# High/low splits of the block products' operands: all subtractions on VectorE, none on GpSimd

## The chip, the cores and the metric

One core of a Trainium2 chip runs the whole program. The metric is the device time of one execution in microseconds (us); shorter is better. The engines are named as in the profile: PE is TensorE's matrix multiply (PEld its weight load), DVE is VectorE, ACT is ScalarE, POOL is GpSimd, SP is the engine whose queue issues most DMAs. Every engine works through its own list of instructions in order; semaphores make it wait for the others.

## The reference

Two layers over 1024 tokens of width 1024, float32, batch 1. Cut to what matters here:

```python
# layer 0: convolution branch and bidirectional RG-LRU branch, then one output projection
z = h @ p["w_in"]                                   # 1024 -> 5 * 1024
y = concat([y_a, y_b], axis=-1) @ p["w_out"]        # 2048 -> 1024
x = x + gate * y
# layer 1: multi-scale pooling mixer
u, g = split(h @ p["w_in"], 2)                      # 1024 -> 2 * 2048
d = multiscale_pool(u)                              # windows 2, 4, 8, 16 along rows of 64 tokens
y = einsum("bngi,gij->bngj", d, p["w_grp"]) * p["scale"]
x = x + gate * ((y * silu(g)) @ p["w_out"])
return rmsnorm(x, final_g)
```

## The kernel before, in words

Features lie on the 128 partitions, tokens along the free axis. TensorE multiplies fp32r operands. To keep float32 accuracy, every operand v is split in two: hi is a copy of v rounded to fp32r, made on ACT, and lo = v - hi, a subtraction (`TENSOR_TENSOR`, line 96) on VectorE or GpSimd. A product is then three matmuls per pair of 128x128 weights and 128x512 data: hi\*hi, hi\*lo, lo\*hi.

From about 764 us to the end of the trace the kernel does "block products", which save multiplications by Strassen's method. Two output rows of 128 features are taken together. Their weights are four blocks a11, a12, a21, a22 (each 128x512), and `wquad` builds seven weight operands `wq_*` from them with one sum and three differences on DVE (L587, L588, L589, L595) and seven splits. The data are cut the same way into b11, b21, b22, t1, t2, t3, t4 (`block_sums` on DVE, L559 to L562). `quad` then runs seven products p1 to p7 (84 matmuls, lines L607, L609, L610) into three PSUM tiles a, c and b. Tile b begins as a copy of a, made on ACT (L625). Results leave PSUM in parts: an ACT copy for a first part, a DVE addition for the second (L1022 and L1030 for the pooling layer, L833, L1077 and L1092 for the output projections). The last product p4 (operand t4) may start adding to b only when DVE has read the part before it.

The order of the products is p1 (b11), p5 (t1), p6 (t2), p2 (b21), p7 (t3), p3 (b22), p4 (t4). The stages are:

- `woa`, 4 quads, about 764 to 862 us: layer 0's output projection. Its data operands `ya` are split by `split_op`.
- about 862 to 906 us: products `fold` of weights for layer 1, normalisation, and the start of the operands `x_*` (`split_x`).
- `v` and `g`, 8 steps of two quads each, about 906 to 1256 us: the pooling input (`v`) and its gate (`g`). In each step DVE also does the pooling sums of two feature rows and two token halves (`pool`: L928 sums, L937 and L941 edges, L946), the gate product (L1062), the block sums of the result, and in four steps two reductions of a 512 KB modulation tile (L206), loaded from DRAM.
- `wo0` and `wo1`, about 1256 to 1446 us: layer 1's output projection in two halves. Its data operands are loaded back from DRAM and split by `y_operand`, 128x1024 at a time.

Which engine subtracts was fixed by hand: in a `wquad` weights 1 and 6 on DVE, weights 2, 3, 4, 5 and 7 on GpSimd; of the data operands about every second one on GpSimd. The raw weights `wr` have two buffers, just one pair, so the next pair is loaded when the splits 3 and 4, the last readers, are done. The order on each engine is set by the framework's scheduler, which plays the program against its own timing model; evictions of PSUM get a raised priority. Changing an engine therefore also reorders the lists.

Of the kernel before, what the change touches and what calls it, by code (L numbers as in the profile page):

```python
# [22 lines left out]
HALF = (slice(0, H), slice(H, S))  # L23
# [32 lines left out]
def body(ctx, tc, xT, ctxT, cc, ccol, modT, modW, win, gw, wout, wu, grp, wg, wo1, small, edge, ident, outT):  # L56
    nc = tc.nc
# [23 lines left out]
    def ttile(name):  # L81
        return tpool.tile([P, H], F32, tag="t", name=name)
# [11 lines left out]
    def split(src, hi, lo, eng):  # L94
        return (nc.scalar.copy(hi, src),  # L95
                eng.tensor_tensor(out=lo, in0=src, in1=hi.bitcast(F32), op=sub))  # L96
# [324 lines left out]
    with ExitStack() as actx:  # L421
# [6 lines left out]
        def ltile(name, dt=F32):  # L428
            return lpool.tile([P, E], dt, tag="l", name=name)
# [49 lines left out]
        for j in range(KT):  # L479
# [15 lines left out]
            for h in range(2):  # L495
                ps = psum(f"vg{j}_{h}")
                mm3(ps, w, (hh, hl), HALF[h])
                t = ttile(f"sg{j}_{h}")
# [16 lines left out]
            for d in range(2):  # L515
                for gi, ob in ((0, O_BR), (1, O_BI)):
                    kc = slice((2 * gi + d) * P, (2 * gi + d + 1) * P)
                    t = ltile(f"g{j}_{d}_{gi}")
# [21 lines left out]
    def vtile(name):  # L540
        return vpool.tile([P, H], F32, tag="v", name=name)
# [10 lines left out]

    def split_op(ops, name, i, src):
        hi, lo = ops[name]
        return split(src, hi[i], lo[i], nc.gpsimd if i % 2 else nc.vector)


    def block_sums(b11, b12, b21, b22, t3, eng):
        eng.tensor_tensor(out=t3, in0=b22, in1=b12, op=sub)  # L559
        eng.tensor_tensor(out=b12, in0=b12, in1=b11, op=sub)  # L560
        eng.tensor_tensor(out=b11, in0=b22, in1=b12, op=sub)
        eng.tensor_tensor(out=b21, in0=b21, in1=b11, op=sub)  # L562
        return dict(t2=b11, t1=b12, t3=t3, t4=b21, b22=b22)
# [5 lines left out]
    def wquad(src, name, ring, late=False):  # L569
        raw = []  # L570
        for i in range(2):
            r = wpool.tile([P, D], F32, tag="wr", name=f"wr_{name}_{i}")
            loaded[0] = nc.sync.dma_start(r, src[i])
            raw.append(r)
        a11, a12 = [raw[0][:, h] for h in HALF]
        a21, a22 = [raw[1][:, h] for h in HALF]

        def op(v, i, eng):
            t = ring(f"wq_{name}_{i}")
            split(v, t[:, HALF[0]], t[:, HALF[1]], eng)  # L580
            return t

        p1 = op(a11, 1, nc.vector)
        if late:
            p4 = op(a22, 4, nc.gpsimd)
        s3 = ttile(f"ws_{name}")
        nc.vector.tensor_tensor(out=s3, in0=a11, in1=a21, op=sub)  # L587
        nc.vector.tensor_tensor(out=a21, in0=a21, in1=a22, op=add)  # L588
        nc.vector.tensor_tensor(out=a11, in0=a21, in1=a11, op=sub)  # L589
        if not late:  # L590
            p5 = op(a21, 5, nc.gpsimd)
        p6 = op(a11, 6, nc.vector)
        p2 = op(a12, 2, nc.gpsimd)
        p7 = op(s3, 7, nc.gpsimd)
        nc.vector.tensor_tensor(out=a12, in0=a12, in1=a11, op=sub)  # L595
        if late:
            p5 = op(a21, 5, nc.gpsimd)
        p3 = op(a12, 3, nc.gpsimd)
        if not late:
            p4 = op(a22, 4, nc.gpsimd)  # L600
        return p1, p2, p3, p4, p5, p6, p7

    def prod(ps, w, op, first, last):
# [109 lines left out]
    for h in range(2):  # L713
        ps = wide(f"mu{h}", h)[:, :H]
        nc.tensor.matmul(ps, ones, lnacc[h][:, :H], start=True, stop=True)
        for j in range(KT):
            v = us[j][:, HALF[h]]
# [3 lines left out]
            else:  # L721
                q = ttile(f"lsq{j}_{h}")
                nc.scalar.activation(q, v, AF.Square)
                eng = nc.gpsimd if h else nc.vector
# [5 lines left out]
    for m in range(KT):  # L730
        w = wload(wout[m, 1], f"wob{m}", nc.gpsimd)
        for h in range(2):
            ps = psum(f"wob{m}_{h}")
            mm3(ps, w, (bh, bl), HALF[h])
            t = vtile(f"xp{m}_{h}")
# [36 lines left out]
    for i in range(KH):  # L772
        for j in (i, KH + i):
            w = wload(win[2 * KT + j], f"ga{j}", nc.gpsimd)
            for h in range(2):
                ps = psum(f"ga{j}_{h}")
                mm3(ps, w, (hh, hl), HALF[h])
                nc.scalar.activation(ps, ps, AF.Silu)
                v = us[j][:, HALF[h]]
                nc.vector.tensor_tensor(out=v, in0=v, in1=ps, op=mult)  # L780
        b11, b12 = [us[i][:, h] for h in HALF]
        b21, b22 = [us[KH + i][:, h] for h in HALF]
        split_op(ya, "b11", i, b11)
        split_op(ya, "b21", i, b21)
        t1, t2, t3, t4 = b11, ttile(f"yat2_{i}"), b12, b21
        nc.vector.tensor_tensor(out=t1, in0=b12, in1=b11, op=sub)
        nc.vector.tensor_tensor(out=t3, in0=b22, in1=b12, op=sub)
        nc.vector.tensor_tensor(out=t2, in0=b22, in1=t1, op=sub)
        nc.vector.tensor_tensor(out=t4, in0=b21, in1=t2, op=sub)
        split_op(ya, "t2", i, t2)  # L790
        split_op(ya, "t1", i, t1)
        for name, v in zip(BOPS[4:], (t3, b22, t4)):
            kept[name].append(v)
        for _ in range((6, 6, 4, 0)[i]):
            next(mods)
# [9 lines left out]
    def wo_weights(m):  # L805
        return wquad([wout[m + i, 0] for i in range(2)], f"woa{m}", ring_w)
# [58 lines left out]
    def v_weights(m, ring):  # L865
        return wquad([wfold[(m + i) // 4][(m + i) % 4].rearrange("p k c -> p (k c)") for i in range(2)], f"v{m}", ring)
# [4 lines left out]
    def split_x(name, i, src, shift, eng):  # L871
        hi, lo = bx[name]
        if shift is None:
            split(src, hi[i], lo[i], eng)
        else:
            nc.scalar.activation(hi[i], src, AF.Identity, bias=shift)
            nc.vector.scalar_tensor_tensor(out=lo[i], in0=src, scalar=shift, in1=hi[i].bitcast(F32), op0=add, op1=sub)

    def scaled(h, k):
        v = x1[k][:, HALF[h]]  # L880
        nc.vector.scalar_tensor_tensor(out=v, in0=v, scalar=a1[:, 0, k : k + 1], in1=rs[h], op0=mult, op1=mult)
        return v

    def shift(k):
        return m1[:, 0, k : k + 1]
# [9 lines left out]
    for i in range(KH):  # L895
        b11, b21 = x1[i][:, HALF[0]], scaled(0, KH + i)
        split_x("b21", i, b21, shift(KH + i), None)
        b12, b22 = scaled(1, i), scaled(1, KH + i)
        t = block_sums(b11, b12, b21, b22, ttile(f"xt3_{i}"), nc.vector)
        split_x("t1", i, t["t1"], None, nc.gpsimd)  # L900
        split_x("t2", i, t["t2"], shift(KH + i), None)
        split_x("t3", i, t["t3"], dsh[:, i : i + 1], None)
        split_x("b22", i, b22, shift(KH + i), None)
        split_x("t4", i, t["t4"], None, nc.gpsimd)


    fin = [None, None]
# [63 lines left out]
    def y_operand(ops, part, name, raw_tile, alloc):  # L971
        hi, lo = [], []
        for q in range(2):
            r = raw_tile(f"yr_{part}_{name}_{q}")
            nc.sync.dma_start(r, y_raw[part][name][:, q * S : (q + 1) * S])
            hi.append(alloc(f"y{part}_{name}h{q}", F32R))
            lo.append(alloc(f"y{part}_{name}l{q}", F32R))
            split(r, hi[q], lo[q], nc.vector if q or name == "b22" else nc.gpsimd)
        halves = lambda ts: [t[:, h] for t in ts for h in HALF]
        ops[name] = halves(hi), halves(lo)  # L980

# [2 lines left out]
    def y_operands(part, raws, names=BOPS, alloc=None):  # L984
        for name in names:
            y_operand(yops[part], part, name, next(raws),
                      alloc or (dtile if name in ("b11", "b21", "t4") else d2tile))
# [11 lines left out]
    def wo1_weights(part, m):  # L999
        return wquad([wo1[m + i, part] for i in range(2)], f"wo{part}_{m}", wo1_ring,  # L1000
                     part == 1 and m >= KT - 4)
# [370 lines left out]
```

## Time and profile before

| | before |
|---|---|
| time, median of 3 runs | 1459.48 us (1458.37 to 1459.95) |
| the profiled execution: time, span | 1463.59 us, 1461.8 us |
| PE busy | 1320.6 us (90%) |
| DVE busy | 1220.5 us (83%), 1389 instructions |
| ACT busy | 653.0 us (45%) |
| POOL busy | 695.8 us (48%), 372 instructions |
| HBM traffic | 124 GB/s over the span |

The span runs from the first to the last instruction of the profiled execution. An engine's busy share over the whole span mixes stages with different limits; what the change is worth is read from 764 us on. A row "A line <- B line: us, times, longest" of the waits says that engine A, before the instruction named, was idle until engine B's instruction named was done. In grouped rows, x is the count, then follow total busy us and the mean ns of one.

### The profile page before, as it was taken

The numbers are of one execution on the slowest core, as the hardware profiler recorded it, in microseconds if no ns is written. First come the engines' busy times: TensorE is split into PE (matmuls) and PEld (weight loads), VectorE is DVE, ScalarE is ACT, GpSimd is POOL, SyncE is SP. The second block draws the span as 40 slices with busy tenths as digits, with TensorE's granted clock in tenths as the row PEclk, the third lists the DMA queues.
The fourth block names the chain that finished last, engine by engine and source line by source line (L and its number), as shares of the span: only waits on it lengthen the run. The fifth ranks groups of instructions, "written<-read, shape, count | busy, mean of one in ns | idle before, by whom it ended". The sixth has DMA issues, their size and how long they took to land. (4 is left out here: it accounts for less than half of the span.)

```text
span 1461.8 us, 15776 instructions
## 1 busy us (share of the span) xinstructions
PE 1320.6 (90%) x5664; PEld 1060.1 (73%) x5664; DVE 1220.5 (83%) x1389; ACT 653.0 (45%) x928; POOL 695.8 (48%) x372
## 2 busy tenths in 40 slices
PE   7889989998899899999998998899889998889796
PEld 4478767776777677788886776677767777668585
DVE  7985889799879899997778749999999887876765
ACT  6343674475467623225424345533333334534442
POOL 5183644663666556424427435543243344654522
PEclk9899999999999999999999999999999999999998
DMA  9731112111211133443545364233323235647623
GB/s 354 253 121 37 65 37 73 51 68 40 79 51 51 64 103 106 142 141 115 168 159 174 121 194 131 86 115 131 127 75 108 101 108 137 234 162 266 237 73 115
DMA packets 82866, 181.79 MB, mean 124 GB/s; under 512 B 7778, under 2 KB 27618, under 8 KB 82788
## 3 DMA queue, kind: packets, MB, share of 16 engines
q1 hardware_dynamic: 74340, 176.60, 35.6%
q10 hardware_dynamic: 8448, 4.20, 1.0%
q8 instruction: 44, 0.72, 0.2%
q14 instruction: 34, 0.28, 0.1%
HBM read 136.72 MB, written 44.04 MB: 124 GB/s over the span
## 5 line engine op out<-in xcount | busy, mean ns | idle before, releaser
L688 DVE SCALAR_TENSOR_TENSOR conv<-u,sm,conv 128x1009 f32<-128x1009 f32 (+14 forms) x240 | 301.0, 1273 | 21.7 <-ACT conv L681 18.5
L96 POOL TENSOR_TENSOR wq_v<-wr_v,wq_v 128x512 fp32r<-128x512 f32 x32 | 54.3, 1712 | 84.6 <-ACT wq_v L95 84.4
L96 POOL TENSOR_TENSOR wq_g<-wr_g,wq_g 128x512 fp32r<-128x512 f32 x32 | 49.8, 1567 | 91.8 <-ACT wq_g L95 91.5
L96 POOL TENSOR_TENSOR wq_wo<-wr_wo,wq_wo 128x512 fp32r<-128x512 f32 x32 | 49.1, 1542 | 58.4 <-ACT wq_wo L95 48.6
L96 POOL TENSOR_TENSOR wl_wu<-wr_wu,wh_wu 128x1024 fp32r<-128x1024 f32 x16 | 39.4, 2467 | 73.6 <-ACT wh_wu L95 73.6
L95 ACT CAST wq_g<-wr_g 128x512 fp32r<-128x512 f32 x48 | 28.2, 619 | 94.7 <-DVE wr_g L588 33.9
L95 ACT CAST wq_v<-wr_v 128x512 fp32r<-128x512 f32 x48 | 28.2, 619 | 81.0 <-DVE wr_v L595 29.3
L521 PE MATMUL g<-uh,wh_gw 128*128 128x512 f32 (+1 forms) x96 | 40.7, 425 | 25.8 <-ACT g L524 16.3
L524 ACT ACTIVATE g<-g,sm 128x512 f32<-128x512 f32 (+1 forms) x96 | 53.6, 624 | 18.0 <-PE g L523 10.0
L440 POOL TENSOR_TENSOR g<-g,uc 128x1280 f32<-128x1280 f32 x16 | 47.4, 2961 | 19.6 <-ACT g L524 19.6
L243 PE MATMUL fold<-gh,wh_wu 128*128 128x512 f32 x128 | 52.7, 413 | 4.3 <-ACT wh_wu L95 4.3
L125 PE MATMUL gb<-h0h,wh_gb 128*128 128x512 f32 x128 | 51.2, 400 | 5.7 <-ACT sb L669 5.7
L244 PE MATMUL fold<-gl,wh_wu 128*128 128x512 f32 x128 | 52.5, 410 | 3.2 <-DVE gl L96 3.2
L95 ACT CAST wq_wo<-wr_wo 128x512 fp32r<-128x512 f32 x48 | 28.8, 619 | 58.9 <-DVE wr_wo L588 15.0
L445 POOL TENSOR_TENSOR g<-g,g 128x1280 f32<-128x1280 f32 x16 | 50.6, 3182 | 9.1 <-ACT g L444 9.1
L446 DVE SCALAR_TENSOR_TENSOR g<-a,g 128x1280 f32<-128x1280 f32 x16 | 37.1, 2317 | 20.4 <-POOL g L445 20.4
L245 PE MATMUL fold<-gh,wl_wu 128*128 128x512 f32 x128 | 50.9, 407 | 2.7 <-POOL wl_wu L96 2.7
L928 DVE TENSOR_TENSOR ws<-ws 128x616 f32<-128x616 f32 (+2 forms) x48 | 52.3, 1091 | 0.9
L458 POOL TENSOR_TENSOR g<-g,g 128x1024 f32<-128x1024 f32 x8 | 19.2, 2394 | 70.6 <-DVE g L455 70.6
L127 PE MATMUL va<-h0h,wl_va 128*128 128x512 f32 x128 | 49.5, 391 | 2.1 <-POOL wl_va L96 2.1
L126 PE MATMUL gb<-h0l,wh_gb 128*128 128x512 f32 x128 | 51.0, 399 | 0.0
L127 PE MATMUL gb<-h0h,wl_gb 128*128 128x512 f32 x128 | 50.8, 398 | 0.0
(566 smaller groups left out, 4744.7 us busy)
## 6 DMA issues: line engine op xcount, KB each, us to landing
mod<-modT SPq DMA_DIRECT2D x28, 512.0 KB, 5.3
wr_wu<-wu SPq DMA_DIRECT2D x16, 512.0 KB, 4.1
x_part<-xp SPq DMA_DIRECT2D x32, 256.0 KB, 2.6
mod<-modT SPq DMA_DIRECT2D x32, 256.0 KB, 3.3
wr_v<-wfold SPq DMA_DIRECT2D x16, 512.0 KB, 3.3
wr_g<-wg SPq DMA_DIRECT2D x16, 512.0 KB, 4.3
yr_t<-y_t SPq DMA_DIRECT2D x16, 512.0 KB, 6.1
wr_wo<-wo SPq DMA_DIRECT2D x16, 512.0 KB, 4.2
```

The source lines that it names most:

```text
L95: return (nc.scalar.copy(hi, src), eng.tensor_tensor(out=lo, in0=src, in1=hi.bitcast(F32), op=sub))
L96: eng.tensor_tensor(out=lo, in0=src, in1=hi.bitcast(F32), op=sub))
L125: nc.tensor.matmul(ps, hi[:, kc], xh[k][:, cols], start=(k == 0), stop=False)
L126: nc.tensor.matmul(ps, hi[:, kc], xl[k][:, cols], start=False, stop=False)
L127: nc.tensor.matmul(ps, lo[:, kc], xh[k][:, cols], start=False, stop=(k == ks - 1))
L243: nc.tensor.matmul(ps, wh[:, kc], gh[i], start=(i == 0), stop=False)
L244: nc.tensor.matmul(ps, wh[:, kc], gl[i], start=False, stop=False)
L245: nc.tensor.matmul(ps, wl[:, kc], gh[i], start=False, stop=(i == 3))
L445: nc.gpsimd.tensor_tensor(out=iu, in0=iu, in1=r, op=mult)
L524: nc.scalar.activation(t[:, a : a + n], ps[:, :n], AF.Sigmoid, bias=col(ob + d * KT + j))
L688: nc.vector.scalar_tensor_tensor(out=acp[:, a:b], in0=us[j][:, a + o : b + o], scalar=col(O_CONVW + 31 * j + k), in1=acp[:, a:b], op0=mult ...
L928: nc.vector.tensor_tensor(out=nxt[:, :, a_:b_], in0=cur[:, :, a_ + o0 : b_ + o0], in1=cur[:, :, a_ + o1 : b_ + o1], op=add)
```

## The change

Every call of `split` in the block products gets VectorE: five of the seven weight splits of a `wquad`, the odd-numbered data operands of `woa`, the operands t1 and t4 of `v`/`g`, and the operands of `wo0`/`wo1` that GpSimd had. In all 174 subtractions move, 162 of 128x512 and 12 of 128x1024. The casts on ACT and the arithmetic stay, and no DMA is added or taken away. GpSimd's list goes from 371 to 197 rows: the earlier stages' work, the splits of `wl_wu`, eight small memsets and the last scaling stay there.

```diff
     def split_op(ops, name, i, src):
         hi, lo = ops[name]
-        return split(src, hi[i], lo[i], nc.gpsimd if i % 2 else nc.vector)
+        return split(src, hi[i], lo[i], nc.vector)
 ...
-        def op(v, i, eng):
+        def op(v, i):
             t = ring(f"wq_{name}_{i}")
-            split(v, t[:, HALF[0]], t[:, HALF[1]], eng)
+            split(v, t[:, HALF[0]], t[:, HALF[1]], nc.vector)
             return t
 ...
-        p1 = op(a11, 1, nc.vector)
+        p1 = op(a11, 1)
 ...
-            p5 = op(a21, 5, nc.gpsimd)
-        p6 = op(a11, 6, nc.vector)
-        p2 = op(a12, 2, nc.gpsimd)
-        p7 = op(s3, 7, nc.gpsimd)
+            p5 = op(a21, 5)
+        p6 = op(a11, 6)
+        p2 = op(a12, 2)
+        p7 = op(s3, 7)
 ...
-        split_x("t1", i, t["t1"], None, nc.gpsimd)
+        split_x("t1", i, t["t1"], None, nc.vector)
 ...
-        split_x("t4", i, t["t4"], None, nc.gpsimd)
+        split_x("t4", i, t["t4"], None, nc.vector)
 ...
-            split(r, hi[q], lo[q], nc.vector if q or name == "b22" else nc.gpsimd)
+            split(r, hi[q], lo[q], nc.vector)
```

Three places show how the lists move; all are in the third step (m = 4) of the `v`/`g` stage. Numbers behind the names tell buffers apart.

First DVE's list, from the last weight sum of `g4` (L589) to the two evictions of `v4` (L1022). Before:

```order
L589 TENSOR_TENSOR wr_g4_0_7259<-wr_g4_1_7261,wr_g4_0_7259 128x512
L928 TENSOR_TENSOR ws4_0_1_7299<-vp0_6540 128x8x79
L96 TENSOR_TENSOR wq_g4_6_7273<-wr_g4_0_7259,wq_g4_6_7273 128x512
L928 TENSOR_TENSOR ws4_0_2_7301<-ws4_0_1_7299 128x8x77
L928 TENSOR_TENSOR ws4_0_4_7303<-ws4_0_2_7301 128x8x73
L595 TENSOR_TENSOR wr_g4_0_7259<-wr_g4_0_7259 128x512
L928 TENSOR_TENSOR ws4_0_8_7305<-ws4_0_4_7303 128x8x65
L937 TENSOR_TENSOR ws4_0_8_7305<-ws4_0_8_7305,eg_117 128x8x8
L941 TENSOR_TENSOR ws4_0_8_7305<-ws4_0_8_7305,eg_117 128x8x7
L946 SCALAR_TENSOR_TENSOR vp0_6540<-ws4_0_8_7305,vp0_6540 128x8x64
L1022 TENSOR_TENSOR vp3_6549<-qb_v4_7156,s1_v4_7182 128x8x64
L1022 TENSOR_TENSOR vp1_6543<-qc_v4_7155,s0_v4_7196 128x8x64
```

The same stretch of DVE's list after the change:

```order
L589 TENSOR_TENSOR wr_g4_0_7259<-wr_g4_1_7261,wr_g4_0_7259 128x512
L96 TENSOR_TENSOR wq_g4_5_7270<-wr_g4_1_7261,wq_g4_5_7270 128x512
L928 TENSOR_TENSOR ws4_0_1_7299<-vp0_6540 128x8x79
L96 TENSOR_TENSOR wq_g4_6_7273<-wr_g4_0_7259,wq_g4_6_7273 128x512
L928 TENSOR_TENSOR ws4_0_2_7301<-ws4_0_1_7299 128x8x77
L96 TENSOR_TENSOR wq_g4_2_7276<-wr_g4_0_7259,wq_g4_2_7276 128x512
L96 TENSOR_TENSOR wq_g4_7_7279<-ws_g4_7266,wq_g4_7_7279 128x512
L928 TENSOR_TENSOR ws4_0_4_7303<-ws4_0_2_7301 128x8x73
L595 TENSOR_TENSOR wr_g4_0_7259<-wr_g4_0_7259 128x512
L928 TENSOR_TENSOR ws4_0_8_7305<-ws4_0_4_7303 128x8x65
L1022 TENSOR_TENSOR vp3_6549<-qb_v4_7156,s1_v4_7182 128x8x64
L1022 TENSOR_TENSOR vp1_6543<-qc_v4_7155,s0_v4_7196 128x8x64
```

Three splits (5, 2, 7) now stand between the weight sums and the evictions, and three pooling instructions (L937, L941, L946) have moved behind the evictions; the splits 3 and 4 follow there too.

Second PE's list, from the end of `v4`'s product p7 (`x_t3`) to the start of its p4 (`x_t4`), with rows left out inside the runs of one product. Before:

```order
L610 MATMUL qb_v4_7156<-x_t3h1_6407,wq_v4_7_7144 128x512
L610 MATMUL qc_v4_7155<-x_b22h0_6410,wq_v4_3_7148 128x512
...
L610 MATMUL qc_v4_7155<-x_b22h1_6411,wq_v4_3_7148 128x512
L607 MATMUL qb_g4_7345<-x_t2h0_6398,wq_g4_6_7273 128x512
...
L609 MATMUL qa_g4_7343<-x_b21l0_6396,wq_g4_2_7276 128x512
L607 MATMUL qb_v4_7156<-x_t4h0_6414,wq_v4_4_7151 128x512
```

And PE's list after the change:

```order
L610 MATMUL qb_v4_7156<-x_t3h1_6407,wq_v4_7_7144 128x512
L609 MATMUL qc_v4_7155<-x_b22l1_6413,wq_v4_3_7148 128x512
L610 MATMUL qc_v4_7155<-x_b22h1_6411,wq_v4_3_7148 128x512
L607 MATMUL qa_g4_7343<-x_b11h0_6390,wq_g4_1_7263 128x512
...
L610 MATMUL qa_g4_7343<-x_b11h1_6391,wq_g4_1_7263 128x512
L607 MATMUL qb_v4_7156<-x_t4h0_6414,wq_v4_4_7151 128x512
```

Between the end of p7 and the start of p4 there were 24 matmuls (7 of p3, 12 and 5 of the next quad); now there are 14 (2 of p3 and the 12 of the next quad's p1).

Third ACT's list, the casts of `g4`'s weights and the copy that starts its tile b. Before:

```order
L95 CAST wq_g4_5_7270<-wr_g4_1_7261 128x512
L95 CAST wq_g4_6_7273<-wr_g4_0_7259 128x512
L95 CAST wq_g4_2_7276<-wr_g4_0_7259 128x512
L95 CAST wq_g4_7_7279<-ws_g4_7266 128x512
L625 COPY qb_g4_7345<-qa_g4_7343 128x512
L95 CAST wq_g4_3_7283<-wr_g4_0_7259 128x512
L95 CAST wq_g4_4_7286<-wr_g4_1_7261 128x512
```

ACT's list after the change, from the cast of weight 7 on:

```order
L95 CAST wq_g4_2_7276<-wr_g4_0_7259 128x512
L95 CAST wq_g4_7_7279<-ws_g4_7266 128x512
L95 CAST wq_g4_3_7283<-wr_g4_0_7259 128x512
L95 CAST wq_g4_4_7286<-wr_g4_1_7261 128x512
L625 COPY qb_g4_7345<-qa_g4_7343 128x512
```

The copy has moved behind the casts 3 and 4, and so behind DVE's L595, which the cast 3 waits for.

On SP's queue the second modulation tile of each of the first four `v`/`g` steps now stands ahead of the two weight loads of the step's `g` quad; before it stood behind both.

More of the change, by code (lines that the diff above doesn't have):

```diff
@@ L576, in wquad @@
         a21, a22 = [raw[1][:, h] for h in HALF]
-        def op(v, i, eng):
+        def op(v, i):
             t = ring(f"wq_{name}_{i}")
-            split(v, t[:, HALF[0]], t[:, HALF[1]], eng)
+            split(v, t[:, HALF[0]], t[:, HALF[1]], nc.vector)
             return t
-        p1 = op(a11, 1, nc.vector)
+        p1 = op(a11, 1)
         if late:
-            p4 = op(a22, 4, nc.gpsimd)
+            p4 = op(a22, 4)
         s3 = ttile(f"ws_{name}")
@@ L590, in wquad @@
         if not late:
-            p5 = op(a21, 5, nc.gpsimd)
-        p6 = op(a11, 6, nc.vector)
-        p2 = op(a12, 2, nc.gpsimd)
-        p7 = op(s3, 7, nc.gpsimd)
+            p5 = op(a21, 5)
+        p6 = op(a11, 6)
+        p2 = op(a12, 2)
+        p7 = op(s3, 7)
         nc.vector.tensor_tensor(out=a12, in0=a12, in1=a11, op=sub)
         if late:
-            p5 = op(a21, 5, nc.gpsimd)
-        p3 = op(a12, 3, nc.gpsimd)
+            p5 = op(a21, 5)
+        p3 = op(a12, 3)
         if not late:
-            p4 = op(a22, 4, nc.gpsimd)
+            p4 = op(a22, 4)
         return p1, p2, p3, p4, p5, p6, p7
```

## The prediction

> **What bounds the kernel now.** I read the page's busy shares first, then the stages by window, then who waits for whom, then single instructions.
>
> ```profile
> span 1461.8 us, 15776 instructions
> PE 1320.6 (90%) x5664; PEld 1060.1 (73%) x5664; DVE 1220.5 (83%) x1389; ACT 653.0 (45%) x928; POOL 695.8 (48%) x372
> ```
>
> By this, DVE looks too full for more work and POOL half empty. The stages say where the change acts (columns: length, then busy us and count of PE, PEld, DVE, ACT, POOL, then the granted PE clock, DMA share, GB/s):
>
> ```profile
> 690.00:764.00 74.00, 74.00 (x329) 61.26 (x328) 58.42 (x129) 27.96 (x41) 22.21 (x11) 1.00 0.50 161
> 764.00:862.00 98.00, 88.31 (x366) 70.13 (x364) 71.43 (x74) 41.52 (x69) 53.38 (x32) 0.95 0.45 147
> 862.00:906.00 44.00, 40.17 (x180) 32.23 (x181) 30.22 (x40) 22.20 (x34) 20.59 (x9) 1.00 0.58 182
> 906.00:1256.00 350.00, 314.67 (x1324) 252.61 (x1323) 311.50 (x399) 133.22 (x233) 146.52 (x96) 0.97 0.35 114
> 1256.00:1395.00 139.00, 121.27 (x496) 97.39 (x496) 104.00 (x94) 60.50 (x91) 75.49 (x42) 0.94 0.62 214
> 1395.00:1462.00 67.00, 53.66 (x257) 44.21 (x255) 41.73 (x66) 22.88 (x42) 19.98 (x17) 0.89 0.27 95
> ```
>
> Up to 764 us the lists are the same but for a few splits, and PE is busy all the time from 690 on. PE's idle time is what can be won: 98 - 88.3 = 9.7 us in woa, 35.3 us in v/g, 17.7 us in wo. In v/g both PE (90%) and DVE (89%) are nearly full. PE's waits there, and the longest of the two other stages (woa, then wo):
>
> ```profile
> PE qb_g L607 <- ACT qb_g L625: 9.6, 3, 4.2
> PE qb_v L607 <- DVE vp L1022: 7.0, 2, 3.9
> PE qb_g L610 <- DVE wq_g L96: 4.7, 2, 3.0
> PE qb_g L607 <- ACT wq_g L95: 4.2, 2, 3.6
> ...
> PE qc_woa L607 <- ACT wq_woa L95: 4.6, 1, 4.6
> ...
> PE qb_wo L607 <- DVE s_wo L1092: 11.3, 3, 6.2
> ```
>
> Nearly all of them are DVE being late: evictions (L1022, L1092), splits (L96), and ACT copies and casts that stand in ACT's list behind casts waiting for DVE's weight sums. POOL is named in none of these. Now the instructions themselves (count, then min/median/max ns):
>
> ```profile
> L1022 DVE TENSOR_TENSOR vp<-qb_v,s_v x8: 677/681/686, 939.4 to 1241.1; 128x512 f32<-128x512 f32 x8
> L96 DVE TENSOR_TENSOR wq_g<-wr_g,wq_g x16: 679/693/1777, 924.3 to 1236.4; 128x512 fp32r<-128x512 f32 x16
> L595 DVE TENSOR_TENSOR wr_g<-wr_g x8: 683/1756/1778, 940.6 to 1238.3; 128x512 f32<-128x512 f32 x8
> L928 DVE TENSOR_TENSOR ws<-vp x32: 803/812/3009, 935.2 to 1248.3; 128x632 f32<-128x632 f32 x32
> L946 DVE SCALAR_TENSOR_TENSOR vp<-ws,vp x32: 674/692/1823, 938.1 to 1253.5; 128x512 f32<-128x512 f32 x32
> L1062 DVE SCALAR_TENSOR_TENSOR y<-vp,sm,y x28: 740/748/1786, 954.1 to 1222.5; 128x512 f32<-128x512 f32 x28
> L96 POOL TENSOR_TENSOR wq_g<-wr_g,wq_g x32: 1262/1630/1933, 935.2 to 1242.3; 128x512 fp32r<-128x512 f32 x32
> ```
>
> An eviction, which has an operand in PSUM, never leaves 0.68 us. The same size with both inputs in SBUF takes either 0.68 or about 1.76 us. The timeline, DVE first and POOL behind it, shows when:
>
> ```profile
> 1063.78 0.69 DVE L96 TENSOR_TENSOR wq_g<-wr_g,wq_g 128x512 fp32r<-128x512 f32 x1
> 1064.39 2.56 DVE L928 TENSOR_TENSOR ws<-ws 128x616 f32<-128x616 f32 x2
> 1066.88 1.78 DVE L595 TENSOR_TENSOR wr_g<-wr_g 128x512 f32<-128x512 f32 x1
> 1068.58 0.69 DVE L928 TENSOR_TENSOR ws<-ws 128x520 f32<-128x520 f32 x1
> ...
> 1070.77 1.66 DVE L946 SCALAR_TENSOR_TENSOR vp<-ws,vp 128x512 f32<-128x512 f32 x1
> 1072.35 0.68 DVE L1022 TENSOR_TENSOR vp<-qb_v,s_v 128x512 f32<-128x512 f32 x1
> 1072.95 0.68 DVE L1022 TENSOR_TENSOR vp<-qc_v,s_v 128x512 f32<-128x512 f32 x1
> ...
> 1064.40 1.93 POOL L96 TENSOR_TENSOR wq_g<-wr_g,wq_g 128x512 fp32r<-128x512 f32 x1 [2.45 <-ACT wq_g L95]
> 1066.30 1.81 POOL L96 TENSOR_TENSOR wq_g<-ws_g,wq_g 128x512 fp32r<-128x512 f32 x1
> 1069.38 2.50 POOL L96 TENSOR_TENSOR wq_g<-wr_g,wq_g 128x512 fp32r<-128x512 f32 x2 [1.28 <-ACT wq_g L95]
> ```
>
> With POOL idle (1063.78, 1068.58) DVE needs 0.69 us; with POOL at a split it needs 1.7 us or so, and POOL is stretched as well, from 1.26 to 1.8 us. They hold each other up. The eviction at 1072.35 came late by just such delays, and PE stood still for it (the shorter of the two L1022 waits, 7.0 - 3.9 = 3.1 us).
>
> **The change, part by part.** *What DVE gains in v/g.* Six groups of that stage (count, busy us, mean ns):
>
> ```profile
> L928 DVE TENSOR_TENSOR ws<-vp 128x632 f32<-128x632 f32 x32 | 34.2, 1074 | 0.5 <-ACT vp L1018 0.2
> L946 DVE SCALAR_TENSOR_TENSOR vp<-ws,vp 128x512 f32<-128x512 f32 x32 | 26.1, 819 | 0.8
> L1062 DVE SCALAR_TENSOR_TENSOR y<-vp,sm,y 128x512 f32<-128x512 f32 x28 | 26.0, 946 | 2.7 <-ACT y L1032 2.7
> L96 DVE TENSOR_TENSOR wq_v<-wr_v,wq_v 128x512 fp32r<-128x512 f32 x15 | 16.9, 1127 | 4.6 <-ACT wq_v L95 4.6
> L96 DVE TENSOR_TENSOR wq_g<-wr_g,wq_g 128x512 fp32r<-128x512 f32 x16 | 15.3, 958 | 1.4 <-ACT wq_g L95 1.4
> L595 DVE TENSOR_TENSOR wr_g<-wr_g 128x512 f32<-128x512 f32 x8 | 10.9, 1360 | 1.8 <-POOL wq_g L96 1.8
> ```
>
> Count times (mean minus the shortest above): 32 x 0.271 = 8.7, 32 x 0.145 = 4.6, 28 x 0.206 = 5.8, 15 x 0.448 = 6.7, 16 x 0.279 = 4.5, 8 x 0.677 = 5.4; together 35.7 us of the 129.4 us busy in them, 28%. With nothing left on POOL in this stage but eight memsets, that goes. The other 182 us hold PSUM readers that gain nothing; bounds for them are 0 and 28% (50 us), and I take 30, since the remaining L928 sums, the next largest work there, are of the stretched kind. Gain 66 us, bounds 36 and 86.
>
> *What DVE gets in v/g.* POOL's 96 instructions in this stage (its row above) are eight memsets and 88 splits: 77 of weights and 8 of x operands of 128x512, and three of 128x1024. At 0.68 us each, or 0.60 from start to start as the two L1022 show, 85 take 51 to 58 us; the three wide ones, at twice 0.68 at most, 4. So DVE gets 55 to 62 and loses 36 to 86: between +26 and -31 us, by my values about -8. DVE's load stays where it was, about 304 of 350 us, though 88 instructions more are on it.
>
> *What the chain gains.* A split took 1.63 us on POOL (median above) behind ACT's cast and now 0.68. Splits 3 and 4 free the two raw weight buffers; only then the next pair is loaded (at 1069.38 the two take 2.50 us, now 1.2 to 1.4). A delayed DVE instruction at the wrong moment no longer adds 1 us before an eviction. Walking back from each PE wait in v/g over the DVE run ahead of it, I find its stretched instructions worth more than the splits put there in nearly all: in the run shown, L928 (1.1), L595 (1.1) and L946 (1.0) lose 3.2 us, against three splits now ahead of L1022 (1.8), while L937, L941 and L946 move behind. The waits do not all end: those behind ACT's L625 and L95 also hang on loads and in-order lists. Bounds are 0 and all 35.3 us of the stage; I take half, 17.6, since the runs' surplus covers about half of the waits.
>
> *woa*, 98 us: 29 moved splits bring 20 us to DVE's 71.4, and stretched work leaves (bounds 0 and 20 us, the 28% again at the top). The first quad needs its splits one after the other; two engines shared them. Its 4.6 us wait hangs on one stretched sum, worth 1.1. Of 9.7 us I take 2, bounds -4 and 9.7 (the lower: eight first splits at 0.68 less the delays of about 1.4 us gone).
>
> *wo*, 139 us: 41 moved splits, about ten of them wide, bring 31 x 0.68 + 10 x 1.36 = 35 us to 104, and about 29 us (28%) leave. The L1092 waits stand behind weight sums on DVE and behind the load of the next weights. Of 17.7 us I take 6, bounds -6 (the balance of 35 and 29) and 17.7.
>
> *Edits worth nothing.* Four or five splits before 764 us lie beside a PE busy 74.0 of 74 us; uncovered they cost 5 x 0.68 = 3.4 us. Four between 862 and 906 lie beside fold products, bounds -3 and +3. Seven or eight after 1395 come to DVE at 41.7 of 67 us; PE works on without them up to 1446 us, and uncovered they cost 5. On SP's queue the second modulation tile passes ahead of the g weights:
>
> ```profile
> mod<-modT SPq DMA_DIRECT2D x28, 512.0 KB, 5.3
> ```
>
> Its 5.3 us would delay the weights in four steps, 21 us if bare; they are first needed after the rest of the v quad, so I take 0.
>
> Sum: 17.6 + 2 + 6 = 25.6, rounded to 25 us. The profiled execution took 1463.6 us, 1.8 outside its span; it would come to 1438.6. The median of the runs is 4.1 us lower, so 1459.5 - 25 = 1434.5 us.
>
> A rule of the Trainium skill speaks against the change: the page Perfetto Trace Analysis, section Optimizing Scalar/DVE Operations, says that when DVE is saturated it may make sense to move work to ScalarE or even GpSimd, and adds that the shared SBUF read port may undo that between those two. By its first half alone the sum would be the first rival's loss; the 0.68 and 1.76 us rows bear out the second half.
>
> **The rivals.** *DVE becomes the bound* (7 in 100). Place: v/g. If the stretching stays, DVE has 311.5 + 55 = 366 us of work in 350: at least 16 us longer, and 55 if its present 38.5 us of idle time stay too; I name 1485 us, with a middle loss of 26. It decides when DVE's load passes 350 us less the idle time that in-order lists force on it; if half of the 38.5 us stays, that is at 331, with a relief under 36 us, which six groups alone give. Against it: POOL has next to nothing left to collide with.
>
> *The eviction wait takes over* (7 in 100). Place: between p7 and p4 of each v/g quad PE's list had 24 matmuls and has 14, at 74.00/329 = 0.225 us each 5.4 and now 3.15 us of cover for L1022, and more splits stand ahead of L1022 on DVE. If all 16 quads lost the 2.25 us, that is 36 us; against the 25 won, 11 slower, 1470 us. It decides from 1.6 us per quad. Against it: DVE reaches L1022 sooner, three pooling instructions having moved behind it.
>
> *PE becomes the only bound* (8 in 100): the 62.7 us of the three stages go except a fifth, 50 us faster, 1409 us. Against it: waits behind loads stay.
>
> *Hidden anyway* (10 in 100): the loop of loading, summing and splitting the weights keeps its length, since 11 instructions of one engine now follow each other where two engines shared them; within 3 us of before, 1459 us, or up to 10 us faster.
>
> **How the numbers follow.** The forecast, 12 to 45 us faster (1414 to 1447), gets 68 in 100; the rivals 7, 7, 8 and 10, of the last 6 within 0.2% (3 us, about what a measurement of this kernel can tell from no change). Faster: 68 + 8 + 4 = 80; same 6; slower 14. Leaving out most of the fast rival (8) and of the slow ones (12), the range is 1412 to 1462 us.
>
> **What would show it.** In the profile after: POOL busy near 0 between 906 and 1256 us; L595 and L928 on DVE at 0.68 and 0.80 in the mean; DVE busy in v/g within 20 us of 304; PE's waits on L1022 and L625 there about halved; the v/g stage 332 us or so long. The prediction is wrong if L928 and L595 keep 1.7 us with POOL idle, if the wait for L1022 comes in most quads, or if casts 3 and 4, standing ahead of L625, make PE wait for that copy.

## The result, and the profile after

The changed kernel takes 1391.24 us (median of 4 runs, 1389.07 to 1391.96), the kernel before on the same chip 1459.72 us (4 runs). The ratio is 0.9527, with a 95% interval of 0.9511 to 0.9544: 68 us, 4.7% faster. The forecast was 25 us, and its range ended at 1412.

The page's first lines of the changed kernel (span; busy time, share and instructions of each engine):

```profile
span 1390.1 us, 15664 instructions
PE 1294.1 (93%) x5664; PEld 1048.9 (75%) x5664; DVE 1175.8 (85%) x1563; ACT 655.2 (47%) x928; POOL 400.6 (29%) x198
```

VectorE has 174 instructions more than before and is busy 44.7 us less. GpSimd loses 295 us.

The stages follow, cut at the first product of woa, of v, of wo and of the last, column-wise product stage. First the kernel before, in the view of windows; the columns are length, busy time of PE, PEld, DVE, ACT and POOL, granted clock, DMA share, GB/s:

```profile
765.10:908.40 143.30, 129.77 (x549) 103.45 (x548) 104.02 (x114) 63.82 (x104) 75.41 (x42) 0.96 0.48 156
908.40:1262.30 353.90, 318.57 (x1334) 255.63 (x1332) 315.37 (x400) 135.16 (x235) 149.97 (x96) 0.97 0.36 115
1262.30:1396.30 134.00, 116.27 (x481) 93.46 (x480) 97.73 (x91) 57.36 (x86) 70.21 (x39) 0.95 0.63 216
1396.30:1461.80 65.50, 52.36 (x251) 43.11 (x249) 41.73 (x66) 22.88 (x42) 19.98 (x17) 0.89 0.28 97
```

The same view of the changed kernel:

```profile
763.70:892.70 129.00, 125.28 (x549) 102.48 (x548) 99.50 (x151) 67.89 (x111) 19.62 (x8) 0.99 0.55 177
892.70:1199.30 306.60, 304.05 (x1333) 249.46 (x1333) 275.78 (x480) 131.09 (x225) 0.95 (x8) 1.00 0.39 130
1199.30:1324.50 125.20, 111.97 (x482) 90.88 (x482) 95.84 (x133) 59.55 (x90) 0.00 (x0) 0.97 0.70 235
1324.50:1390.10 65.60, 51.49 (x251) 42.53 (x249) 43.80 (x74) 22.70 (x42) 8.26 (x9) 0.91 0.29 97
```

These are the profiled executions, 71.7 us apart in span; that of the kernel before took 1463.59 us, 3.9 us above the median given here. Woa with the fold became 14.3 us shorter, v/g 47.3, wo 8.8, the tail not. Two columns say where it came from. TensorE's idle time, length less busy time, fell by 9.8, 32.8 and 4.5 us. Its *busy* time for the same matmuls fell too, by 4.5, 14.5 and 4.3 us, and the granted clock rose to 0.99, 1.00 and 0.97. In v/g only 2.5 us of idle time are left; the stage stands on TensorE's own 304 us.

TensorE's waits in the v/g stage of the changed kernel (total, times, longest), where before ACT's copy L625, the eviction L1022 and the casts stood:

```profile
PE qb_v L607 <- DVE vp L1022: 1.0, 1, 1.0
PE qc_v L607 <- ACT s_v L653: 0.7, 1, 0.7
PE qb_g L607 <- DVE y L1030: 0.6, 2, 0.3
PE qc_v L609 <- DVE x_t1l L96: 0.4, 1, 0.4
```

VectorE's groups in the changed kernel (count, busy us and mean ns, idle time before):

```profile
L96 DVE TENSOR_TENSOR wq_g<-wr_g,wq_g 128x512 fp32r<-128x512 f32 x48 | 32.3, 685 | 7.2 <-ACT wq_g L95 7.2
L928 DVE TENSOR_TENSOR ws<-vp 128x632 f32<-128x632 f32 x32 | 25.7, 808 | 0.0
L595 DVE TENSOR_TENSOR wr_g<-wr_g 128x512 f32<-128x512 f32 x8 | 5.5, 682 | 0.0
```

Every form of 512 elements and more that the stage has in both kernels has come down to within 10 ns of its shortest duration of before: in the mean 808 instead of 1074 ns, 682 instead of 1360.

### The profile page after: what moved, and what is told of

The parts are those of the page before. It is cut to its first block, busy times and chain, and to the rows that moved or that the text cites. A ratio compares the mean times of both kernels' runs of the same rounds, so it can differ in the third digit from the quotient of the medians.

```text
span 1390.1 us, 15664 instructions
## 1 busy us (share of the span) xinstructions
PE 1294.1 (93%) x5664; PEld 1048.9 (75%) x5664; DVE 1175.8 (85%) x1563; ACT 655.2 (47%) x928; POOL 400.6 (29%) x198
## 4 chain that ended last, share of the span: by engine, by line
PE 39%; DVE 33%; DMA 9%; ACT 8%; issue 6%; POOL 4%; SPq 0%; POOLq 0%; DVEq 0%; ACTq 0%
DVE conv L688 6%; DVE g L455 2%; DVE ws L928 2%; DMA wr_g<-wg 2%; DVE mod L206 1%; DVE junk L206 1%; DMA wr_v<-wfold 1%; DMA mod<-modT 1%; PE fold L245 1%; DMA x_part<-xp 1%; PE fold L244 1%; PE fold L243 1%; DVE wq_v L96 1%; DVE wq_g L96 1%; ACT g L524 1%
## 5 line engine op out<-in xcount | busy, mean ns | idle before, releaser
L688 DVE SCALAR_TENSOR_TENSOR conv<-u,sm,conv 128x1009 f32<-128x1009 f32 (+14 forms) x240 | 300.9, 1272 | 21.9 <-ACT conv L681 18.7
L1192 POOL TENSOR_TENSOR o<-x,rr 128x256 f32<-128x256 f32 (+1 forms) x9 | 8.3, 944 | 461.1 <-ACT rr L1180 458.9
L440 POOL TENSOR_TENSOR g<-g,uc 128x1280 f32<-128x1280 f32 x16 | 47.3, 2957 | 19.8 <-ACT g L524 19.8
L95 ACT CAST wq_wo<-wr_wo 128x512 fp32r<-128x512 f32 x48 | 28.9, 619 | 46.5 <-DMA wr_wo<-wo 16.6
L126 PE MATMUL wob<-ybl,wh_wob 128*128 128x512 f32 x128 | 50.3, 394 | 0.0
L127 PE MATMUL ga<-h0h,wl_ga 128*128 128x512 f32 x128 | 50.2, 392 | 0.0
L127 PE MATMUL xb<-h0h,wl_xb 128*128 128x512 f32 x128 | 50.1, 391 | 0.0
L125 PE MATMUL xb<-h0h,wh_xb 128*128 128x512 f32 x128 | 50.0, 391 | 0.0
L127 PE MATMUL wob<-ybh,wl_wob 128*128 128x512 f32 x128 | 50.0, 393 | 0.0
L125 PE MATMUL wob<-ybh,wh_wob 128*128 128x512 f32 x128 | 49.9, 394 | 0.0
```

The costliest lines, as they stand in the source:

```text
L125: nc.tensor.matmul(ps, hi[:, kc], xh[k][:, cols], start=(k == 0), stop=False)
L126: nc.tensor.matmul(ps, hi[:, kc], xl[k][:, cols], start=False, stop=False)
L127: nc.tensor.matmul(ps, lo[:, kc], xh[k][:, cols], start=False, stop=(k == ks - 1))
L440: nc.gpsimd.tensor_tensor(out=ius[d], in0=ius[d], in1=uc, op=mult)
L688: nc.vector.scalar_tensor_tensor(out=acp[:, a:b], in0=us[j][:, a + o : b + o], scalar=col(O_CONVW + 31 * j + k), in1=acp[:, a:b], op0=mult ...
```

## Experiments

Theory 1: VectorE work with two SBUF operands and GpSimd work that reads SBUF delay each other, and the change took this away. Rival: the gain is the splits' shorter and reordered path, or plainly VectorE's load. A third theory concerns size: TensorE's waits also cost clock after them.

**x1, the collisions alone brought back.** A spare tile is added, and at each of the 174 moved splits GpSimd does this; all else stays.

```diff
+        nc.gpsimd.tensor_tensor(out=jt, in0=hi.bitcast(F32), in1=hi.bitcast(F32), op=sub)
```

> The changed kernel with its splits left on VectorE; beside each of the 174 moved splits GpSimd now reads the split's high half as both operands of a subtraction into a spare tile that nobody uses (extra work, the outputs are unchanged). The instruction lists of TensorE, VectorE, ScalarE and SyncE stay row for row those of the changed kernel, so only the collisions come back. Theory 1 (two-operand work on VectorE and GpSimd work that reads SBUF stretch each other): VectorE's 276 us in the v/g stage grow by 60 to 85 us, the stage passes its 307 us to 345 to 380, and the time is 1440 to 1490 us. Rival (the gain is the shorter and reordered path of the splits and the empty GpSimd queue): within 5 us of 1391. Third theory, clock slots lost behind TensorE's waits: they return here, TensorE's busy time in the v/g stage goes from 304 to about 315 us.

Measured: 1477.1 us, ratio to before 1.0104 (1.0086 to 1.0123). With the changed kernel's lists on every other engine it is slower than the kernel before. Its v/g stage in the view of windows:

```profile
904.30:1266.00 361.70, 322.03 (x1333) 257.65 (x1331) 343.40 (x479) 129.31 (x225) 140.75 (x101) 0.96 0.33 109
```

Its groups of splits on VectorE and of the added work on GpSimd:

```profile
L96 DVE TENSOR_TENSOR wq_g<-wr_g,wq_g 128x512 fp32r<-128x512 f32 x48 | 47.7, 1006 | 4.0 <-ACT wq_g L95 3.9
L542 POOL TENSOR_TENSOR jt<-wq_g 128x512 bf16<-128x512 f32 x40 | 58.2, 1454 | 104.7 <-ACT wq_g L95 102.9
```

The split goes from 685 to 1006 ns, VectorE's busy time in v/g grows by 67.6 us, TensorE's idle time from 2.5 to 39.7 us and its busy time by 18.0. The order of the instructions on TensorE, VectorE and ScalarE is that of the changed kernel throughout, and no instruction of the trace waits for the added work: the shorter and reordered path as the whole cause is out. How much of the 68 us the new order gave by itself, no run separates.

**x2, GpSimd as busy, but hardly reading.**

```diff
+        nc.gpsimd.tensor_copy(out=jt[:, :1], in_=hi[:, :1].bitcast(F32))
+        for _ in range(3): nc.gpsimd.memset(jt, 0.0)
```

> The same, but at each moved split GpSimd reads only one column of the high half and then fills the spare tile three times (extra work, outputs unchanged), so that it is busy at the same places for about as long and reads next to nothing from SBUF. Lists of the other engines as in the changed kernel. Theory 1, collisions need a GpSimd instruction that reads SBUF: within 5 us of 1391, VectorE's split of 512 columns at 0.68 us and its pooling addition at 0.81. If any GpSimd work hinders VectorE (writes too, or a busy GpSimd): 1430 or more.

Measured: 1390.93 us, 0.9516 (0.9497 to 0.9536), the changed kernel's time. Its v/g stage:

```profile
895.50:1200.80 305.30, 304.00 (x1333) 249.39 (x1332) 276.77 (x481) 132.23 (x225) 222.37 (x376) 1.00 0.39 131
```

The groups of VectorE's splits and of GpSimd's fillings:

```profile
L96 DVE TENSOR_TENSOR wq_g<-wr_g,wq_g 128x512 fp32r<-128x512 f32 x48 | 32.3, 686 | 5.3 <-ACT wq_g L95 4.5 <-PE qc_v L622 0.6
...
L542 POOL MEMSET jt<- 128x512 bf16 x558 | 293.1, 525 | 32.2
```

GpSimd is busy for 222 of 305 us, more than in x1, and costs nothing. It is the reading that matters. Together x1 and x2 settle theory 1: the same places and the same lists, and 86 us between them.

**x3, one operand read instead of two.** As x1 with `tensor_copy(out=jt, in_=hi)`.

> The same, but at each moved split GpSimd copies the high half into the spare tile: one operand read from SBUF instead of two (extra work, outputs unchanged). Lists of the other engines as in the changed kernel. If a collision is an exclusive hold for as long as GpSimd's instruction runs, the loss against the changed kernel is that of the two-operand run scaled by the copy's duration to the subtraction's: with a copy of about 0.8 of the duration, 1425 to 1475. If only two-operand reads on both sides collide: within 5 us of 1391. Rival of the shorter path: 1391.

Measured: 1420.97 us, 0.9721 (0.9704 to 0.9737). Its v/g stage:

```profile
896.00:1221.40 325.40, 309.27 (x1333) 251.15 (x1332) 304.95 (x481) 130.88 (x225) 100.72 (x100) 0.99 0.37 122
```

One group of GpSimd's copies:

```profile
L541 POOL CAST jt<-wq_g 128x512 bf16<-128x512 f32 x40 | 48.2, 1204 | 97.8 <-ACT wq_g L95 96.5
```

One read collides too, so it isn't only two against two. But 1421 lies 4 us under the expected range: the loss against the changed kernel is 30 us where the copy's median of 0.95 us against the subtraction's 1.37 would give 59. VectorE lost 29 us in v/g, 0.43 of x1's 68, and the stage 18.8 us, 0.34 of x1's 55.1. How these fractions come about stays open.

**e2, a smaller dose.** Products 3 and 4, the last wanted, back on GpSimd.

```diff
-            split(v, t[:, HALF[0]], t[:, HALF[1]], nc.vector)
+            split(v, t[:, HALF[0]], t[:, HALF[1]], nc.gpsimd if i in (3, 4) else nc.vector)
```

> The change for all operand splits and for products 2, 5 and 7 of each weight quad; products 3 and 4, the last wanted, stay on GpSimd (56 of the 174 moved splits go back). If each GpSimd split costs its share (174 splits, 68 us): 22 us back, 1413, range 1405 to 1420. If what mattered was that the late splits delayed TensorE through a long path, these last-wanted two cost little: 1391 to 1398. If the loss is a threshold (waits come only once the lead of the quads is used up): also 1391 to 1400, with VectorE stretched but TensorE's waits in the v/g stage under 10 us.

Measured: 1397.31 us, 0.9563 (0.9544 to 0.9581). Its v/g stage:

```profile
892.10:1207.40 315.30, 306.34 (x1333) 248.82 (x1332) 282.58 (x447) 129.76 (x225) 53.62 (x40) 1.00 0.38 126
```

TensorE's longest group of waits there:

```profile
PE qb_v L607 <- DVE vp L1022: 6.6, 5, 2.2
```

A third of the moved splits went back, but only 6 of the 68 us. VectorE has 33 instructions fewer in v/g (some 20 us at 0.61 us each, the step from one to the next) and is still busy 7 us longer, so about 27 us of stretching are back. TensorE idles 9.0 us instead of 2.5, and the stage is 8.7 us longer. The loss does not go with the number of splits: GpSimd also took those 20 us off VectorE again, and what the stage lost is close to the 7 us net. Whether the lists take up the first stretching, or whether it counted that these two are wanted last, this run doesn't tell apart.

**e3, the opposite direction.** All seven weight splits on GpSimd (`nc.gpsimd` in place of `nc.vector` in that line), operands on VectorE.

> The opposite direction: operand splits on VectorE as in the changed kernel, but all seven weight splits of a quad on GpSimd, the two that VectorE had in the kernel before among them (196 weight splits there). If what counts is VectorE's load (it was busy for 315 of 354 us in the v/g stage), this takes work from it and the time is 1440 or less. Theory 1, each GpSimd split costs VectorE more in collisions (about 0.9 us by the 85 us of stretching over 96 splits) than the 0.68 us that it takes over: no shorter than before, 1455 to 1490.

Measured: 1452.5 us, 0.994 (0.992 to 0.9961). Its stages woa with fold, and v/g:

```profile
763.80:898.60 134.80, 127.21 (x550) 103.08 (x549) 101.05 (x115) 64.99 (x106) 71.08 (x40) 0.97 0.53 166
898.60:1252.30 353.70, 321.12 (x1333) 259.06 (x1331) 302.75 (x376) 130.52 (x229) 166.42 (x115) 0.95 0.35 113
```

In v/g VectorE is busy 12.6 us less than in the kernel before, and the stage is as long as it was, 353.7 against 353.9 us: less load on VectorE won nothing there. The time fell 2.5 us under my range: 8.5 of the 10.7 us won between the profiled executions lie in woa and fold. Their operand splits came to VectorE, but that this is the reason is not shown.

**e4, stage by stage.** The weight splits of woa and wo as before, the rest as changed.

```diff
+            split(..., nc.gpsimd if i in (2, 3, 4, 5, 7) and name[0] not in "vg" else nc.vector)
```

> The change without its weight splits in the two other stages: the five weight splits of each woa and wo quad are on GpSimd as before (60 of the 174), the weights of v and g and all operand splits are on VectorE. If the stages gain each by its own collisions: v/g keeps its 47 us, and of the 14 us of woa and fold and the 9 us of wo about the share of these splits is lost, 10 to 20 us in all, 1400 to 1412. If v/g gained through what earlier or later stages hand on to it, its stage of 307 us becomes longer by over 5.

Measured: 1406.41 us, 0.9621 (0.96 to 0.9642). Its stages, woa with fold to the end:

```profile
762.00:897.70 135.70, 128.81 (x550) 104.32 (x549) 103.98 (x129) 67.83 (x110) 50.45 (x28) 0.96 0.53 169
897.70:1207.70 310.00, 304.71 (x1334) 249.30 (x1333) 276.93 (x482) 131.37 (x227) 0.95 (x8) 1.00 0.39 129
1207.70:1344.10 136.40, 119.99 (x505) 97.64 (x504) 99.36 (x106) 61.91 (x93) 51.42 (x33) 0.95 0.63 215
1344.10:1404.10 60.00, 46.91 (x227) 38.61 (x225) 37.17 (x61) 20.07 (x39) 18.23 (x16) 0.88 0.31 105
```

V/g keeps all but 3.4 us of its gain; woa with fold loses 6.7 us, wo and tail together 5.6. The stages gain each by itself.

**e5, waits of TensorE without collisions.** In the v quads the eviction L1022 is made late by ScalarE, and the g quad's first product may not fill the gap.

```diff
+                if i == 1:
+                    for _ in range(4): nc.scalar.copy(x, x)
                 nc.vector.tensor_tensor(out=token[i][h], in0=rows(x), in1=rows(parts[i]), op=add)
...
+            if name[0] == "g":
+                pin.enter_context(tc.issue_after(p4_end[0].ins))
             prod(a, p1, ops["b11"], True, False)
```

> The changed kernel with waits made on TensorE by another means than collisions: in the eight v quads ScalarE copies the PSUM block onto itself four times before the last but one eviction (extra work, outputs unchanged), and the first product of the g quad that follows is held behind product 4 of the v quad, so that only two matmuls lie between product 7 and the product 4 that waits for this eviction. Each v quad should wait about 4 x 0.6 + 0.68 = 3.1 us more, eight of them 20 to 30 us of idle TensorE in the v/g stage. GpSimd stays idle there and VectorE's 276 us stay. Theory of the clock (idle time of TensorE also costs speed of the matmuls that follow): the 1333 matmuls of the stage take 8 to 12 us more than 304 (from the runs so far, 0.35 to 0.45 us for each us of idle time), and the kernel is longer than 1391 by idle plus that, about 1420 to 1430. Rival (the slower matmuls of the kernel before came from the collisions themselves or from shared memory traffic, not from the waits): the 304 us stay within 2 and the kernel is longer by the idle time alone.

Measured: 1449.36 us, 0.9915 (0.9896 to 0.9934). Its v/g stage:

```profile
893.50:1263.70 370.20, 322.60 (x1333) 261.12 (x1332) 285.38 (x483) 148.12 (x260) 0.95 (x8) 0.93 0.33 108
```

Three stretches of 5 us around one of its waits, in the same columns:

```profile
960.00:965.00 5.00, 1.58 (x7) 0.96 (x6) 5.00 (x11) 2.86 (x7) 0.00 (x0) 0.88 0.00 0
965.00:970.00 5.00, 2.20 (x5) 1.81 (x6) 3.60 (x8) 1.03 (x2) 0.00 (x0) 0.50 0.66 209
970.00:975.00 5.00, 5.00 (x22) 4.04 (x22) 2.19 (x4) 1.23 (x3) 0.00 (x0) 0.94 0.00 1
```

The waits came out larger than meant, 47.6 us of idle time instead of 20 to 30, of which 45.9 in eight waits of 4.2 to 7.2 us. With GpSimd at rest the same matmuls took 18.6 us more than in the changed kernel, 0.39 us for each us of idle time. The clock is granted at 0.50 where TensorE starts again. So slow matmuls follow from the waits, not from collisions.

**e6, the same waits, short.** E5 without the four copies.

> The stall kernel again, with its first product of the g quad held behind product 4 of the v quad but without the four extra copies, so that the wait in each v quad is shorter by about 4 x 0.6 = 2.4 us: from 4.2 to 7.2 us before, to 2 to 4 us now. In the runs so far matmuls after a wait of over 3.2 us started at a granted clock of 0.50 and lost 1.4 to 3 us over the next 24, and after waits under 2.8 us mostly 0.1 to 0.2. Theory of a threshold of about 3 us: waits that come out under it cost only themselves; with eight waits of 2 to 2.8 us the stage's 1333 matmuls stay at 304 to 307 us and the time is 1391 + 16 to 22, about 1410. If the loss goes with idle time whatever its pieces (0.41 us for each us in the stall kernel): 311 to 314 us, and about 1420. If most waits stay over 3.2 us: about 320 us again and 1430.

Measured: 1403.69 us, 0.96 (0.9565 to 0.9634). Its v/g stage:

```profile
890.20:1215.20 325.00, 309.54 (x1333) 251.40 (x1332) 281.65 (x483) 131.14 (x227) 0.95 (x8) 0.99 0.37 123
```

The group of waits that the edit made (total, times, longest):

```profile
PE qb_v L607 <- DVE vp L1026: 12.6, 8, 2.8
```

The waits were 0.4 to 2.8 us, below what I had meant, and the 309.5 us of busy time lie between the two theories. Wait by wait it is clearer. Six of the eight, 0.4 to 1.8 us, were each followed by 24 matmuls with 0.1 us of delay in all; the two longest, 2.4 and 2.8 us, by 1.7 us each, with seven matmuls recorded at 0.63 instead of 0.39 us. My threshold of about 3 us was too high and too sharp. Over the 13 traces of this study, from woa to the end of wo, for waits with no other within 24 matmuls (a wait counted from the end of one recorded matmul to the start of the next; slow where at least five of the next 24 took over 0.55 us; the delay is taken against the 5.44 us that 24 matmuls take without a wait):

| wait of TensorE | number | followed by slow matmuls | mean delay in these |
|---|---|---|---|
| 0.35 to 1.5 us | 46 | 0 | |
| 1.5 to 3.5 us | 49 | 24 | 1.9 us |
| over 3.5 us | 35 | 35 | 2.1 us |

Three tries to win more follow. **i1** puts all weight splits of the earlier stages on VectorE too (`nc.vector` in each `wload`), and the context's sums of squares.

> The changed kernel, and beyond it all weight splits of the stages ahead (recurrence inputs, gates, projections, the folded weights) on VectorE instead of GpSimd, and the sums of the context's squares. About 58 splits of 1024 columns at 1.22 us and 8 of 512 at 0.68 come to VectorE, some 75 us over a stretch in which it is busy for about 600 of 764 us. Theory 1: collisions with these GpSimd splits go too, TensorE's waits for them there (10 us) go, and the time falls by 5 to 15 us, to 1376 to 1386. Rival, VectorE is the bound of the recurrence and of the convolution (taps of 300 us that read PSUM and did not stretch), so the added work shows: 1400 to 1440.

Measured: 1415.47 us, 0.9683 (0.9666 to 0.97), 24 us more than the changed kernel. Its time ahead of woa:

```profile
0.00:779.90 779.90, 698.33 (x3055) 562.30 (x3056) 709.04 (x798) 371.37 (x459) 217.96 (x102) 0.95 0.32 107
```

Two of TensorE's new waits there:

```profile
PE ga L125 <- DVE u L780: 12.8, 1, 12.8
...
PE ms_ln L175 <- DVE lnsum L725: 10.2, 1, 10.2
```

The rival was right: 16 us of the loss lie there, where VectorE is the busy engine; the other 8 are spread over the later stages, and no run says why. VectorE's long convolution (L688) has one operand in PSUM and had nothing to gain: in the kernel before, 149 of its 240 taps had a reading GpSimd instruction beside them for at least a fifth of their time and took 1.27 us in the median, the same as the other 91. The same kind of edit that wins 68 us later loses here.

**i2** takes away the changed kernel's longest wait in wo (7.4 us on the copy L625, behind casts that wait for loads) by issuing six operand splits, each a cast and its subtraction, later.

```diff
+            if part == 1 and name in ("t3", "b22", "t4"): late.append((r, hi[q], lo[q]))   # split in ahead()
```

> A try to beat the changed kernel: in its last product stage the six ScalarE casts of the operand blocks t3, b22 and t4, which wait for loads, are issued behind the copy that starts the second accumulator of the first quad, instead of three of them ahead of it. The changed kernel's longest wait of TensorE, 7.4 us on this copy (a wait over 3 us, so that the matmuls behind it also lost 1.6 us), should shrink to 3 or less: 4 to 8 us off, 1383 to 1387. Rival: the copy then waits for casts of weights 3 and 4 or the product of t3 waits for its late operand, and the time stays within 2 us of 1391.

Measured: 1392.16 us, 0.9519 (0.9486 to 0.9552): no gain. That wait is gone, and TensorE's waits in wo and after it now begin with these:

```profile
PE qb_wo L607 <- DVE s_wo L1096: 5.2, 2, 3.5
PE qa_wo L607 <- DVE xp L1081: 3.4, 1, 3.4
```

**i3** moves only the recurrence's projection weights (`xb`) to VectorE.

> The second try: beyond the change only the eight weight splits of the recurrence's own projection (1024 columns each) go from GpSimd to VectorE; TensorE waited 7.4 us in four waits of at most 2.1 us for them. If the wait is what counts: 3 to 7 us off, 1384 to 1388. If VectorE bounds the recurrence, as in the run with all weight splits there (16 us lost ahead of woa by some 75 us more work, 0.2 us for each us): 8 x 1.22 = 10 us more work cost about 2 us, 1391 to 1394.

Measured: 1387.09 us, 0.9486 (0.9451 to 0.9521), which overlaps the changed kernel's interval: a gain of 4 us is not shown. The 7.4 us of waits for `wl_xb` went, but those for the convolution behind it rose from 6.7 us to this row:

```profile
PE g L521 <- DVE uc L487: 16.9, 6, 3.9
```

## Why the prediction was wrong

*The direction and the mechanism of the collisions* held. POOL has 0.95 us in v/g, L595 and L928 stand at 0.68 and 0.81, and x1 and x2 show the collisions as the cause.

*The term mis-sized: "half of the 35.3 us" in v/g, 17.6.* Measured were 32.8 us of idle time. I took half because the waits behind L625 and L95 also hang on loads and in-order lists, and because the surplus of VectorE's runs covered about half of the waits. The loads and lists held nothing up, and VectorE's relief was larger than I took: I had its load about 8 us lower, and it fell by 39.6, from 315.4 us to 275.8. With 80 instructions more (49 us at 0.61 each) this means that about 88 us of stretching went, against my 66; compared form by form it is 84. X1, with the changed kernel's lists and the stretching back, idles 39.7 us, so in these lists the idle time hangs on the stretching. The mark "DVE busy in v/g within 20 us of 304" failed with it, and the waits on L1022 and L625 did not halve but went to 1.0 us and none. In the other stages I took 2 for woa and nothing for the fold where 9.8 of idle time went; for wo 6, with 4.5 found.

*The term left out: the clock.* My bound of 62.7 us for all three stages counted idle time alone. TensorE's busy time fell by 23.3 us more, of the 70.4 us of the three stages. The rows with the granted clock of 0.95, 0.97 and 0.94 stood in the rows of the stages that I showed; I made no term of them. E5 shows that waits alone slow the matmuls behind them. The same is seen here: in the three stages 99 matmuls of the kernel before were recorded at over 0.55 us, and 19 of the changed kernel; the spacing of their starts beyond the regular 0.227 us adds up to 21 and 4 us, so this makes up about 17 of the 23.3. Idle time (47.1) and busy time (23.3) together are the 70.4 us, of which I had 25.6 and nothing.

*The rivals.* "PE becomes the only bound" came true in v/g, 306.6 us for 304 of matmuls, but at 1409 it too lacked the clock. "DVE becomes the bound" fell: 276 of 307 us. "The eviction wait takes over" fell at 14 matmuls of cover, 1.0 us in all; e6 shows what two leave, 12.6 us over eight quads. "Hidden anyway" fell.

*Edits costed at nothing* held where they could be seen: the time ahead of woa was 1.4 us shorter, the tail 65.5 and 65.6 us. The reordered modulation tile cost nothing: no wait of TensorE in v/g ends on a load.

*The rule weighed there* (the Trainium skill, Perfetto Trace Analysis, Optimizing Scalar/DVE Operations): its first half, to move work of a busy VectorE to GpSimd, does not hold in v/g, where e3 gave GpSimd more weight splits and the stage stayed at 353.7 us, and the change took all away and won 47.3. Ahead of woa it holds: i1 took such work back and lost 16 us there. Its second half, that the shared port may undo the gain, agrees with v/g, where VectorE's instructions beside the splits have two SBUF operands.

## What to carry to other kernels

Before giving work to GpSimd, look at what VectorE does beside it: in this kernel two-operand SBUF work there paid for GpSimd's reads (up to 1.78 instead of 0.68 us), while PSUM-fed work didn't (1.27 us either way). Compare an instruction's longest with its shortest duration. When waits of TensorE go, count the matmuls' own slowness behind waits of over 1.5 to 3.5 us as well, about 2 us each, by the granted clock of the stage. When the engine that causes the waits gets a large relief, do not halve them without a reason: here 32.8 of 35.3 us went, and the stage came down to its matmuls' busy time at a granted clock of 1.00.

## What the runs showed of the hardware

- GpSimd's read can be held up long. In x2 a copy of one column, 0.19 us at its shortest, took 6.94 us, while VectorE ran eleven two-operand instructions back to back at 0.68 to 0.69 us, undisturbed. GpSimd's rows in the timeline (start, duration):

```profile
886.64 6.94 POOL L540 CAST jt<-wq_v 128x1 bf16<-128x1 f32 x1 [9.62 <-ACT wq_v L95]
893.63 1.11 POOL L542 MEMSET jt<- 128x512 bf16 x2
```

  Two of VectorE's rows beside them:

```profile
887.42 0.69 DVE L601 TENSOR_TENSOR wr_v<-wr_v,wr_v 128x512 f32<-128x512 f32 x1
...
892.84 0.69 DVE L96 TENSOR_TENSOR wq_v<-wr_v,wq_v 128x512 fp32r<-128x512 f32 x1
```

  The Trainium skill, SBUF — State Buffer, SBUF: two separate sides, calls the pair of ports an exclusive lock, held for a whole instruction, taken by a VectorE instruction with two SBUF inputs only against GpSimd work that reads SBUF. X2's memsets beside undisturbed splits agree with the last part, and this row with the lock; that whoever starts first gets it does not explain eleven turns in a row for VectorE.
- A wait of TensorE has a price beyond its length, with a soft edge: of the waits in the table none under 1.5 us, half of those up to 3.5 us (24 of 49) and all 35 above were followed by slow matmuls, which lost 1.9 and 2.1 us in the mean. The Trainium skill, TensorE: Matmul & The Clock Gate, Why this matters for your kernels, advises no gaps of over about 3 us. The waits over 3.5 us agree; the slow starts after shorter ones, 1.5 us on, do not.
